# The opening of a two-layer MLP kernel: first weight group loaded and used in pieces between the x tiles, filler bank reused, transposes in two banks

## The chip, the core and the metric

The program runs on one core of one Trainium2 chip. The metric is the device time of one execution in microseconds (us); lower is better. The runs of the kernel before took 876.52 to 876.78 us, with a median of 876.71 us over three.

## What is computed

x has 16 x 512 rows of 768, w1 is 768 x 3072, w2 is 3072 x 768; all of it is float32.

```python
y = np.matmul(x, w1) + b1
y = 0.5 * y * (1.0 + erf(y / np.sqrt(2.0)))
return np.matmul(y, w2).astype(np.float32)
```

## The kernel before, in words

The 8192 rows are cut into pairs of two halves of up to 384 rows. For each pair the kernel forms the hidden values g (first product, bias, Gelu) and then the output (second product). From the second pair on, the first product uses Strassen-like sums with 7 products in place of 8 (function product1, L154), and the second product uses a 15-product scheme (part2, L229). All that needs sums of weights made on the chip. In the opening, where no such sums exist yet, the first pair is computed plainly: w1 is loaded in eight groups of 3 x 128 columns (load_w1), and for each group and half of the rows the function plain (L400) issues six matmuls of 128x384, one for each 128-row chunk of K, into one PSUM bank, and Gelu reads the bank.

PSUM has 8 banks, handed out in turn by bank(), which waits until the earlier user of a bank is done. All matrix instructions run on TensorE (PE) in the order in which the program issues them, since every instruction is recorded as in order.

Before the plain groups 1 to 7 comes the part that the change touches. It handles group 0 of w1 and the six 128-row tiles of x of the first pair:

- x tiles 0 and 1 are loaded by SP's queue as float32 (into xw) and cast to bf16 by DVE and ACT. b1 is loaded on ACT's queue. x tiles 2 to 5 (load_x0) and all weights (load_w1, load_w2) are loaded by POOL's queue, which converts to bf16 on the way. Its order is: x tile 2; chunks 0 to 2 of w1 group 0; then POOL makes the identity matrix (masks.py:197 and 199, cast at L106); chunks 3 to 5 of group 0; x tiles 3, 4, 5; group 1 in two halves; then groups 2 to 7 with the pieces of w2 between them. At most eight of POOL's DMAs are under way: from the ninth on, an issue waits until the DMA eight places ahead of it has landed.
- While nothing has landed, busy(n) (L411) issues n filler matmuls of 128x512 on zeros into a bank pw. There are 9, then 1 and 2 more between the transposes.
- turn_x0(n) (L426) transposes tile n with six PE instructions into a new bank, and DVE copies the result to xt (L104). A small transpose of b1 (L492), copied by ACT, stands between tiles 1 and 2.
- first(n, k0, k1) (L464) multiplies tile n (128 rows) with chunks k0 to k1 of group 0, for its three column blocks: 18 matmuls of 128x128 for one tile with all six chunks. Three tiles of a half share a bank for each column block; Gelu for a half's three banks follows when its last tile is done.

The order on PE is: tiles 0 to 2 transposed, fillers, chunks 0 to 2 for tiles 0 to 2, chunks 3 to 5 for tile 0, transpose of tile 3, chunks 3 to 5 for tiles 1 and 2, transpose of tile 4, tile 3, transpose of tile 5, tile 4, tile 5, then plain.

Of the kernel before, what the change touches and what calls it, by code (L numbers as in the profile page):

```python
# [9 lines left out]
BF16 = mybir.dt.bfloat16  # L10
ACTF = mybir.ActivationFunctionType
ALU = mybir.AluOpType
P = 128
# [20 lines left out]
def kernel(  # L34
# [8 lines left out]
    nc = tc.nc  # L43
# [5 lines left out]
    KC = K // P  # L49
    HC = H // P  # L50
    HP = HC // 2
    KH = KC // 2
    NB = N // 2
    HW = 384
# [20 lines left out]
    def inorder(ins):  # L75
        return tc.keep_in_program_order(ins)

    def dma(queue, out, in_):
        inorder(queue.dma_start(out=out, in_=in_))  # L79
# [9 lines left out]
    xt = keep.tile([P, KC, 2, HW], BF16, name="xt")  # L89
# [5 lines left out]
    b1t = keep.tile([P, HC], FP32, name="b1t")  # L95

    def bank():
        return psp.tile([P, 512], FP32, name="ps")

    def copy(engine, dst, src):  # L100
        if engine == "act":
            inorder(nc.scalar.copy(out=dst, in_=src))  # L102
        elif engine == "dve":
            inorder(nc.vector.tensor_copy(out=dst, in_=src))  # L104
        else:
            inorder(nc.gpsimd.tensor_copy(out=dst, in_=src))  # L106
# [24 lines left out]
    def place_h(hc):  # L131
        h, j = divmod(hc, HP)
        k, q = divmod(j, QH)
        return k * QC + h * QH + q
# [7 lines left out]
    def gelu1(hc, half, src, w, sign):  # L142
        inorder(nc.scalar.activation(out=g[:, place_h(hc), half, :w], in_=src, func=ACTF.Gelu,  # L143
                                     bias=b1t[:, hc:hc + 1], scale=sign))
# [133 lines left out]
    def place(w, n):  # L278
        ns = w // P
        return n // ns, (n % ns) * P  # L280
# [47 lines left out]
    def w1_pair(q):  # L328
        return xftf if HOME[q] is None else w1t[:, HOME[q]:HOME[q] + 2 * GRP]

    def w1_group(gi):
        return w1_pair(gi // 2)[:, gi % 2 * GRP:(gi % 2 + 1) * GRP].rearrange("p (kc c) -> p kc c", kc=KC)

    def load_w1(gi, k0=0, k1=KC):
        c0 = (gi % 2 * HP + gi // 2 * 3) * P
        dma(nc.gpsimd, out=w1_group(gi)[:, k0:k1, :], in_=w1r[:, k0:k1, c0:c0 + 3 * P])
# [70 lines left out]
    pw = bank()  # L407

    def busy(n):
        for _ in range(n):  # L410
            inorder(nc.tensor.matmul(out=pw[:], lhsT=warm[:, 0:P], rhs=warm, start=True, stop=True))  # L411


    def words(ap, first, count):
        return ap[:, 2 * first:2 * (first + count)].bitcast(FP32)
# [4 lines left out]
    def load_x0(n):  # L420
        dma(nc.gpsimd, out=xb0[:, n, :], in_=xf[n * P:(n + 1) * P, :])

    def turn_x0(n, engine):
        pt = bank()[:, :KC * P // 2].bitcast(BF16).rearrange("p (kc c) -> p kc c", kc=KC)
        for kc in range(KC):
            inorder(nc.tensor.transpose(out=pt[:, kc, :], in_=xb0[:, n, kc * P:(kc + 1) * P], identity=ident))  # L426
        half, c0 = place(HW, n)
        copy(engine, xt[:, :, half, c0:c0 + P], pt)

    b1s = words(stf, 2304, P)[:HC, :]  # L430
    ident32 = words(stf, 2432, P)
# [2 lines left out]
    dma(nc.sync, out=xw[:, 1, :], in_=xf[P:2 * P, :])  # L434
    dma(nc.scalar, out=b1s, in_=b1.rearrange("(hc p) -> hc p", p=P))
    load_x0(2)
    load_w1(0, 0, KH)
    inorder(nc.vector.memset(warm, 0.0))
    inorder(nc.scalar.activation(out=b1t[:, 0:1], in_=warm[:, 0:1], func=ACTF.Gelu))
    busy(9)  # L440
    make_identity(nc, ident32)
    copy("pool", ident, ident32)
    load_w1(0, KH, KC)
    for n in range(3, 6):
        load_x0(n)
    load_w1(1, 0, KH)
    load_w1(1, KH, KC)
    load_w1(2)
# [5 lines left out]

    opened = {}

    def first(n, k0=0, k1=KC):
        half, c0 = place(HW, n)
        for hc in range(3):
            if c0 == 0 and k0 == 0:  # L460
                opened[half, hc] = bank()
            ps = opened[half, hc]
            for kc in range(k0, k1):
                inorder(nc.tensor.matmul(out=ps[:, c0:c0 + P], lhsT=w1_group(0)[:, kc, hc * P:(hc + 1) * P],  # L464
                                         rhs=xt[:, kc, half, c0:c0 + P], start=(c0 == 0 and kc == 0),
                                         stop=(kc == KC - 1), skip_group_check=True))
            if c0 == HW - P and k1 == KC:
                gelu1(hc, half, ps[:, :HW], HW, 1.0)

    def groups(p):  # L470
        nonlocal spare, turn
# [11 lines left out]
    EARLY = ("M2a", "M3a")  # L483
    MIDDLE = ("M12", "M2b", "M10a", "M11a", "M11b")

    copy("dve", xb0[:, 0, :], xw[:, 0, :])
    turn_x0(0, "dve")
    copy("act", xb0[:, 1, :], xw[:, 1, :])
    busy(1)
    turn_x0(1, "dve")  # L490
    tb = bank()
    inorder(nc.tensor.transpose(out=tb[:, :HC], in_=b1s, identity=ident32[:HC, :HC]))  # L492
    copy("act", b1t[:], tb[:, :HC])
    turn_x0(2, "dve")
    busy(2)
    for n in range(3):
        first(n, 0, KH)
    first(0, KH, KC)
    turn_x0(3, "dve")
    first(1, KH, KC)  # L500
    first(2, KH, KC)
    for n in range(3, 6):
        if n < 5:
            turn_x0(n + 1, "dve")
        first(n)

    def plains(gi):
        for n in range(3):
# [59 lines left out]
    for p, (r0, w) in enumerate(pairs):  # L568
# [123 lines left out]
        else:  # L692
# [7 lines left out]
            for n, c0, c1 in ((0, 0, NB), (1, 0, NB // 2), (1, NB // 2, NB)):  # L700
                terms = halves[n]
                ps = bank()
                for f, lhs in terms:
                    for c in range(QC):
                        inorder(nc.tensor.matmul(  # L705
                            out=ps[:, :c1 - c0], lhsT=lhs[:, c, :], rhs=w2t[:, c, WF[f], c0:c1],
                            start=(f == terms[0][0] and c == 0), stop=(f == terms[2][0] and c == QC - 1)))
# [33 lines left out]
```

## Time and profile before

| what | value |
|---|---|
| time of the profiled execution | 876.7 us |
| its span (first to last instruction) | 874.9 us |
| median of the runs (lowest, highest) | 876.71 us (876.52, 876.78) |
| PE busy | 868.7 us, 99% of the span |
| DVE, ACT, POOL busy | 591.1, 399.9, 84.4 us |
| first matmul of group 0 (L464) starts | 8.59 us |
| first plain matmul (L400) starts | 16.05 us |

How to read it: all times in the trace count from the first instruction of the span. 1.8 us of the time lie outside the span. A row of the timeline gives the start, the length, the engine, the line, what is written and read, how many instructions are merged, and in brackets how long the engine was idle before it and what ended that. A matmul's end is modelled and lies behind the point at which the next one can start, so the spacing of starts is the better measure of what PE can do. The time to landing of a DMA counts from its issue to the last of its parts being in place.

### The profile page before, as it was taken

The numbers are of one execution on the slowest core, as the hardware profiler recorded it, in microseconds if no ns is written. First come the engines' busy times: TensorE is split into PE (matmuls) and PEld (weight loads), VectorE is DVE, ScalarE is ACT, GpSimd is POOL, SyncE is SP. The second block draws the span as 40 slices with busy tenths as digits, with TensorE's granted clock in tenths as the row PEclk, the third lists the DMA queues.
The fourth block names the chain that finished last, engine by engine and source line by source line (L and its number), as shares of the span: only waits on it lengthen the run. The fifth ranks groups of instructions, "written<-read, shape, count | busy, mean of one in ns | idle before, by whom it ended". The sixth has DMA issues, their size and how long they took to land.

```text
span 874.9 us, 14162 instructions
## 1 busy us (share of the span) xinstructions
PE 868.7 (99%) x5524; PEld 533.8 (61%) x5524; DVE 591.1 (68%) x1110; ACT 399.9 (46%) x792; POOL 84.4 (10%) x153
## 2 busy tenths in 40 slices
PE   8999999999999999999999999999999999999998
PEld 5666566666666666666666666666666666666775
DVE  2889868657856676676577556756765776577654
ACT  3742484167127614731671276147316712751560
POOL 6200110010110001000101100010001011000000
PEclk9999999999999999999999999999999999999999
DMA  9997699276627735671767277366718662771521
GB/s 196 207 209 234 219 324 227 78 204 213 161 64 230 214 89 156 216 170 73 217 204 157 68 240 202 87 166 208 171 71 229 195 153 77 234 196 55 189 88 73
DMA packets 89319, 148.00 MB, mean 169 GB/s; under 512 B 50828, under 2 KB 68388, under 8 KB 89252
## 3 DMA queue, kind: packets, MB, share of 16 engines
q1 hardware_dynamic: 64976, 97.04, 37.2%
q0 software_dynamic: 24096, 49.36, 23.7%
q8 instruction: 43, 0.70, 0.3%
q10 hardware_dynamic: 180, 0.70, 0.2%
q14 instruction: 24, 0.20, 0.1%
HBM read 123.88 MB, written 33.42 MB: 180 GB/s over the span
## 4 chain that ended last, share of the span: by engine, by line
PE 98%; DMA 1%; DVE 0%; POOL 0%; issue 0%; ACT 0%; DVEq 0%; POOLq 0%
PE ps L229 47%; PE ps L154 45%; PE ps L400 5%; PE ps L705 1%; DMA st<-in_x_dram 1%; PE ps L464 0%; POOL w1t L79 0%; PE ps L426 0%; DVE ps L112 0%; DVE ev L112 0%; DVE ev L104 0%; DVE g L112 0%; DVE st L112 0%; POOL st L79 0%; ACT ot L102 0%
## 5 line engine op out<-in xcount | busy, mean ns | idle before, releaser
L154 PEld LDWEIGHTS <-w1t 128*128 128x128 bf16 x2436 | 238.3, 98 | 145.2 <-issue 0.8
L143 ACT ACTIVATE g<-ps,b1t 128x384 bf16<-128x384 f32 (+1 forms) x409 | 221.9, 569 | 89.3 <-PE ps L154 56.8
L154 PE MATMUL ps<-xft,w1t 128*128 128x384 bf16 (+1 forms) x1392 | 259.7, 320 | 0.0
L229 PE MATMUL ps<-w2t,g 128*128 128x384 bf16 x1512 | 257.6, 326 | 0.0
L229 PEld LDWEIGHTS <-g 128*128 128x128 bf16 x1512 | 148.0, 98 | 97.3
L154 PE MATMUL ps<-xt,w1t 128*128 128x384 bf16 (+1 forms) x1044 | 202.3, 320 | 0.1
L109 DVE TENSOR_TENSOR ot<-ot,ps 128x384 f32<-128x384 f32 x231 | 125.5, 552 | 107.4 <-PE ps L229 51.1
L229 PE MATMUL ps<-w2t,st 128*128 128x384 bf16 x1008 | 170.7, 326 | 0.0
L102 ACT COPY ot<-ps 128x384 f32<-128x384 f32 x129 | 60.9, 477 | 220.9 <-PE ps L229 202.6
L229 PEld LDWEIGHTS <-st 128*128 128x128 bf16 x1008 | 98.6, 98 | 65.2
L112 DVE TENSOR_TENSOR ev<-ps,ev 128x384 f32<-128x384 f32 (+1 forms) x119 | 64.7, 544 | 74.6 <-PE ps L154 72.8
L102 ACT COPY ps<-ps 128x384 f32<-128x384 f32 (+1 forms) x119 | 54.0, 454 | 132.9 <-PE ps L154 132.7
L112 DVE TENSOR_TENSOR ps<-ps,ev 128x384 f32<-128x384 f32 (+1 forms) x119 | 65.8, 553 | 44.2 <-PE ps L154 42.1
L104 DVE COPY ev<-ps 128x384 f32<-128x384 f32 (+1 forms) x119 | 64.3, 541 | 22.2 <-PE ps L154 22.0
L143 ACT ACTIVATE g<-ev,b1t 128x384 bf16<-128x384 f32 (+1 forms) x119 | 72.1, 606 | 14.8 <-DVE ev L112 14.7
L112 DVE TENSOR_TENSOR st<-g 128x1024 bf16<-128x1024 bf16 x107 | 73.0, 683 | 1.1 <-ACT g L143 0.9
L79 POOL DMA_DIRECT2D out_dram<-ot x60 | 32.6, 544 | 340.1 <-DVE ot L109 340.1
L112 DVE TENSOR_TENSOR g<-g 128x1024 bf16<-128x1024 bf16 x84 | 57.5, 684 | 0.4
L79 POOL DMA_DIRECT2D xb<-in_x_dram x38 | 20.6, 548 | 341.1 <-DMA xt<-xb 334.3
L400 PE MATMUL ps<-xt,w1t 128*128 128x384 bf16 x204 | 33.8, 326 | 0.0
L109 DVE TENSOR_TENSOR g<-g 128x1024 bf16<-128x1024 bf16 x42 | 29.0, 690 | 1.1
L109 DVE TENSOR_TENSOR st<-st,g 128x1024 bf16<-128x1024 bf16 x42 | 28.9, 688 | 0.8
(73 smaller groups left out, 259.5 us busy)
## 6 DMA issues: line engine op xcount, KB each, us to landing
w1t<-w1f SPq DMA_DIRECT2D x116, 672.0 KB, 5.3
out_dram<-ot POOLq DMA_DIRECT2D x60, 384.0 KB, 2.6
xb<-in_x_dram POOLq DMA_DIRECT2D x38, 192.0 KB, 4.7
w2t<-in_w_dram POOLq DMA_DIRECT2D x8, 576.0 KB, 22.3
ot<-in_x_dram POOLq DMA_DIRECT2D x18, 192.0 KB, 7.7
w1t<-in_w_dram POOLq DMA_DIRECT2D x4, 576.0 KB, 22.2
w1f<-st POOLq DMA_DIRECT2D x3, 672.0 KB, 3.8
w1f<-ot POOLq DMA_DIRECT2D x3, 672.0 KB, 9.1
```

The lines of the kernel that those rows point to most:

```text
L79: inorder(queue.dma_start(out=out, in_=in_))
L102: inorder(nc.scalar.copy(out=dst, in_=src))
L104: inorder(nc.vector.tensor_copy(out=dst, in_=src))
L109: inorder(nc.vector.tensor_tensor(out=dst, in0=a, in1=b, op=ALU.add))
L112: inorder(nc.vector.tensor_tensor(out=dst, in0=a, in1=b, op=ALU.subtract))
L143: inorder(nc.scalar.activation(out=g[:, place_h(hc), half, :w], in_=src, func=ACTF.Gelu, bias=b1t[:, hc:hc + 1], scale=sign))
L154: inorder(nc.tensor.matmul(out=ps[:, :w], lhsT=forms[:, W1F[m], kc, :], rhs=moving1(m, kc, w), start=(kc == 0 and m in ("P1", "P7")), stop ...
L229: inorder(nc.tensor.matmul(out=ps[:, :NB], lhsT=lhs[:, c, :], rhs=w2t[:, c, WF[m], :], start=(m in OPENS and c == 0), stop=(c == QC - 1), ...
L400: inorder(nc.tensor.matmul(out=py[:, :HW], lhsT=lhs[:, kc, (j % 3) * P:(j % 3 + 1) * P], rhs=xt[:, kc, half, :], start=(kc == 0), stop=(kc ...
L705: inorder(nc.tensor.matmul(out=ps[:, :c1 - c0], lhsT=lhs[:, c, :], rhs=w2t[:, c, WF[f], c0:c1], start=(f == terms[0][0] and c == 0), stop= ...
```

## The change

Group 0 of w1 is loaded as five DMAs (chunks 0 and 1 together, then 2, 3, 4, 5 alone) in place of two, and x tiles 3, 4 and 5 are issued between them. The function first now takes a half, a range of its columns (rows of x) and a range of chunks: tiles 0 to 2 are multiplied together, in matmuls of 128x384, chunk by chunk as the pieces arrive; tiles 3 to 5 keep matmuls of 128x128. Nine fillers stay ahead of tile 0, with b1's transpose after the seventh of them; one filler each follows tiles 0 and 1, and two follow tile 2. The filler bank pw becomes the bank of the first sum of half 0. All six tiles are transposed in two fixed banks, turn about; b1's transpose uses a free corner of the second.

```diff
+    turns = (bank(), bank())
+
     def turn_x0(n, engine):
-        pt = bank()[:, :KC * P // 2].bitcast(BF16).rearrange("p (kc c) -> p kc c", kc=KC)
+        pt = turns[n % 2][:, :KC * P // 2].bitcast(BF16).rearrange("p (kc c) -> p kc c", kc=KC)
...
     load_x0(2)
-    load_w1(0, 0, KH)
+    load_w1(0, 0, 2)
     inorder(nc.vector.memset(warm, 0.0))
     inorder(nc.scalar.activation(out=b1t[:, 0:1], in_=warm[:, 0:1], func=ACTF.Gelu))
-    busy(9)
     make_identity(nc, ident32)
     copy("pool", ident, ident32)
-    load_w1(0, KH, KC)
-    for n in range(3, 6):
-        load_x0(n)
+    load_x0(3)
+    load_w1(0, 2, 3)
+    load_w1(0, 3, 4)
+    load_x0(4)
+    load_w1(0, 4, 5)
+    load_x0(5)
+    load_w1(0, 5, 6)
     load_w1(1, 0, KH)
     load_w1(1, KH, KC)
...
-    def first(n, k0=0, k1=KC):
-        half, c0 = place(HW, n)
-        for hc in range(3):
-            if c0 == 0 and k0 == 0:
-                opened[half, hc] = bank()
-            ps = opened[half, hc]
-            for kc in range(k0, k1):
-                inorder(nc.tensor.matmul(out=ps[:, c0:c0 + P], lhsT=w1_group(0)[:, kc, hc * P:(hc + 1) * P],
-                                         rhs=xt[:, kc, half, c0:c0 + P], start=(c0 == 0 and kc == 0),
+    def first(half, c0, c1, k0, k1):
+        if c0 == 0 and k0 == 0:
+            for hc in range(3):
+                opened[half, hc] = pw if half == 0 and hc == 0 else bank()
+        for kc in range(k0, k1):
+            for hc in range(3):
+                inorder(nc.tensor.matmul(out=opened[half, hc][:, c0:c1], lhsT=w1_group(0)[:, kc, hc * P:(hc + 1) * P],
+                                         rhs=xt[:, kc, half, c0:c1], start=(c0 == 0 and kc == 0),
                                          stop=(kc == KC - 1), skip_group_check=True))
-            if c0 == HW - P and k1 == KC:
-                gelu1(hc, half, ps[:, :HW], HW, 1.0)
+        if c1 == HW and k1 == KC:
+            for hc in range(3):
+                gelu1(hc, half, opened[half, hc][:, :HW], HW, 1.0)
...
+    busy(7)
+    tb = turns[1][:, 448:448 + HC]
+    inorder(nc.tensor.transpose(out=tb, in_=b1s, identity=ident32[:HC, :HC]))
+    copy("act", b1t[:], tb)
+    busy(2)
     copy("dve", xb0[:, 0, :], xw[:, 0, :])
     turn_x0(0, "dve")
     copy("act", xb0[:, 1, :], xw[:, 1, :])
     busy(1)
     turn_x0(1, "dve")
-    tb = bank()
-    inorder(nc.tensor.transpose(out=tb[:, :HC], in_=b1s, identity=ident32[:HC, :HC]))
-    copy("act", b1t[:], tb[:, :HC])
+    busy(1)
     turn_x0(2, "dve")
     busy(2)
-    for n in range(3):
-        first(n, 0, KH)
-    first(0, KH, KC)
+    first(0, 0, HW, 0, 2)
     turn_x0(3, "dve")
-    first(1, KH, KC)
-    first(2, KH, KC)
-    for n in range(3, 6):
-        if n < 5:
-            turn_x0(n + 1, "dve")
-        first(n)
+    first(0, 0, HW, 2, 3)
+    first(1, 0, P, 0, 3)
+    first(0, 0, HW, 3, 4)
+    first(1, 0, P, 3, 4)
+    turn_x0(4, "dve")
+    first(0, 0, HW, 4, 5)
+    first(1, 0, P, 4, 5)
+    first(1, P, 2 * P, 0, 3)
+    turn_x0(5, "dve")
+    first(1, P, 2 * P, 3, 5)
+    first(0, 0, HW, 5, 6)
+    first(1, 0, P, 5, 6)
+    first(1, P, 2 * P, 5, 6)
+    first(1, 2 * P, HW, 0, 6)
```

## The prediction

> **What bounds the kernel now.** I read the page's chain first, then PE's waits over the whole span, then the timeline of the first 22 us.
>
> ```profile
> span 874.9 us, 14162 instructions
> ...
> PE 98%; DMA 1%; DVE 0%; POOL 0%; issue 0%; ACT 0%; DVEq 0%; POOLq 0%
> ```
>
> ```profile
> PE ps L411 <- DVE st L438: 1.2, 1, 1.2
> PE ps L464 <- DMA w1t<-in_w_dram: 1.2, 1, 1.2
> PE ps L426 <- ACT st L102: 0.4, 1, 0.4
> PE ps L426 <- DMA st<-in_x_dram: 0.2, 1, 0.2
> ```
>
> The chain that ends last is PE nearly throughout, and PE's only listed waits in 874.9 us (who, for what, total, times, longest) are these four, all in the opening. So the end moves by as much as the first plain matmul (L400, 16.05 us) moves, unless something later becomes late. What sets the 16.05 is in PE's timeline:
>
> ```profile
> 1.19 3.56 PE L411 MATMUL ps<-st 128*128 128x512 bf16 x9 [1.19 <-DVE st L438]
> 4.78 0.51 PE L426 MATMUL ps<-st 128*128 128x128 bf16 x6
> ...
> 5.87 0.51 PE L426 MATMUL ps<-st 128*128 128x128 bf16 x6 [0.37 <-ACT st L102]
> ...
> 6.82 0.59 PE L411 MATMUL ps<-st 128*128 128x512 bf16 x2
> 8.59 2.18 PE L464 MATMUL ps<-xt,w1t 128*128 128x128 bf16 x36 [1.17 <-DMA w1t<-in_w_dram]
> 11.01 0.51 PE L426 MATMUL ps<-st 128*128 128x128 bf16 x6 [0.24 <-DMA st<-in_x_dram]
> ...
> 12.36 0.50 PE L426 MATMUL ps<-st 128*128 128x128 bf16 x6
> ...
> 14.04 2.17 PE L464 MATMUL ps<-xt,w1t 128*128 128x128 bf16 x36
> 16.05 6.01 PE L400 MATMUL ps<-xt,w1t 128*128 128x384 bf16 x36
> 21.90 1.30 PE L400 MATMUL ps<-xt,xft 128*128 128x384 bf16 x7
> ```
>
> Real work starts at 8.59, when half of group 0 has landed. From there PE needs 7.05 us of work and loses 0.41 (36 x 0.0558 after 8.59 is 10.60; the next start is 11.01, when x tile 3 has landed): 8.59 + 7.05 + 0.41 = 16.05.
>
> Durations, by spacing of starts: a 128x128 matmul (16.05 - 14.04)/36 = 0.0558 us; a 128x384 one (21.90 - 16.05)/36 = 0.1625; six transposes 12.70 - 12.36 = 0.34. From the start of a tile's transposes until PE may use it:
>
> ```profile
> 12.90 0.56 DVE L104 COPY xt<-ps 128x768 bf16<-128x768 bf16 x1 [0.78 <-PE ps L426]
> ```
>
> 12.90 + 0.56 - 12.36 = 1.10, and 0.06 to wake PE (DVE's cast ends at 4.72, PE starts at 4.78): **1.16 us**.
>
> **The transfers.** From the second microsecond on the DMA engines always have a backlog: landings follow bytes. POOL's issues, with the times to landing that the trace gives for their windows:
>
> ```profile
> 1.92 0.78 POOL L79 DMA_DIRECT2D w1t<-in_w_dram  x1
> ...
> 3.57 0.79 POOL L79 DMA_DIRECT2D w1t<-in_w_dram  x1
> 4.36 1.65 POOL L79 DMA_DIRECT2D st<-in_x_dram  x3
> 5.98 1.53 POOL L79 DMA_DIRECT2D w1t<-in_w_dram  x2
> ```
>
> ```profile
> DMA to landing us min/median/max: 6.6/7.0/7.4
> ```
>
> The last line is that of the three x tiles. Half 1 of group 0: 1.92 + 6.6 = 8.52 (PE wakes 0.07 later). Half 2: 3.57 + 6.5 = 10.07. x tiles 3 to 5: 4.36 + 6.6 = 10.96, about 11.9, and 12.9. First half of group 1: 5.98 + 8.4 = 14.4; second: 15.8. So 288 KB (bf16 as stored) of w1 take 1.5 us, 192 KB of x 0.95: 0.5 us per 96 KB for both, with nothing visible per DMA (0.95 x 1.5 = 1.43 against 1.5). How a DMA of 96 KB, one chunk, behaves, the trace does not show. Bounds: 0.5 by its bytes, 0.95 if it costs as much as the smallest POOL load shown, an x tile. Less than 0.5 is excluded by the steady rate. I take **0.5**, since two sizes lie on one line through zero.
>
> The pieces then land at: chunks 0 and 1, 8.52 - 0.50 = 8.02; x3 8.97; chunk 2 9.47; chunk 3 9.97; x4 10.92; chunk 4 11.42; x5 12.37; chunk 5 12.87. That is the same total as before (x5 at 12.9), in another order. Issue is no limit: x3 now goes out before half 2 did, three more issues at 0.55 to 0.79 leave POOL free near 8, over 4 us ahead of the data, and the wait for the DMA eight places ahead puts group 1's first half at 8.3 (behind 8.02) in place of 5.98, with four loads of x and w1 still queued. From the load of group 5 on, the issues are those of before (14.66, behind the landing at 14.4).
>
> Queued x tiles land 0.95 us apart, so no DMA here holds up the next by more than that. The Trainium skill (DMA: Bandwidth & Descriptors, section "Anatomy of one DMA — SWDGE (gpsimd) path") speaks against small DMAs: it gives about 2.0 us fixed for each DMA on this path, most of it the wait for the write's receipt, beside bytes at 436 GB/s. If these times followed one another, three more DMAs would by that page of the Trainium skill make an estimated 6 us; by the trace they overlap.
>
> **Edits that cost nothing.** b1's transpose before tile 0: b1's packets are all moved by 3.1 us and the identity it needs is made at 3.28 (2.99 + 0.29), while PE reaches it after seven fillers at about 4.2. It takes 0.17 (6.31 to 6.48) in place of nothing, and tile 0 waits for DVE until 4.78 anyway. If the two fillers behind it still ran at the cold spacing (0.43), tile 0 would start at 5.2; tile 1 still waits for ACT's cast until 5.87, so nothing behind moves. ACT now copies b1t before that cast: done by about 4.9, and the cast waits for its x tile until 4.98. Queued behind it is only the cast; if it were late, tiles 1 and 2 would be late by the same amount, with 0.4 us of cover before 8.09. Two banks for the transposes: each is reused two tiles later, when DVE has long copied it. The filler bank as a sum's bank: PE writes both, in order. The plain groups get their banks back from the last transposes and from half 0's Gelu (now about 14.4 to 16; the third plain bank is wanted at 17.5).
>
> **The sum on PE.** Chunks 0 and 1 on tiles 0 to 2: start 8.02 + 0.07 = 8.09 (tiles 0 to 2 are ready at about 7.6), 6 x 0.1625, to 9.07. x3 landed: transposes to 9.41, tile 3 usable at 9.07 + 1.16 = 10.23. Chunk 2: 9.47 + 0.07 = 9.54 (**0.13 lost**), 0.49, to 10.03. Tile 3, chunks 0 to 2: waits to 10.23 (**0.20 lost**), 9 x 0.0558, to 10.73. Chunk 3: 0.49 + 0.17, to 11.39. Tile 4's transposes, to 11.73, usable 12.55. Chunk 4: 0.49 + 0.17, to 12.39. Tile 4, chunks 0 to 2: waits to 12.55 (**0.16 lost**), to 13.05. Tile 5's transposes, to 13.39. Then 0.34, chunk 5 (0.49 + 0.17 + 0.17), to 14.56, tile 5 usable since 14.21; 18 x 0.0558, to **15.56**. Before: 16.05, so **0.49 us** earlier. The wait for the first half shrinks by 0.50, the one for x3 goes, and 0.49 of new small waits is paid, two of them for the trip through DVE; wide matmuls save 54 x 0.0558 - 18 x 0.1625 = 0.09.
>
> What is late next: group 1's first half, landed at 14.4 (cover 1.2 us). Group 2 landed at 7.50 + 11.3 = 18.8 and is wanted at 21.4; group 7 at 24.78 + 22.9 = 47.7, wanted near 50.7. The instructions after the opening stand in the same order on every engine. So the whole 0.49 should arrive at the end: the profiled time 876.7 (874.9 + 1.8 outside; the median is the same 876.71) less 0.5 is **876.2 us**.
>
> **Rivals.** (1) *Nothing of the new small waits is real*, because pieces land sooner than the slowest of before: PE starts when tiles 0 to 2 are ready, about 7.65, and has 6.95 us of work: 14.6 at the earliest, 1.45 less, 875.25; halfway, 875.7. For it: 2.5 us pass from x tile 2's landing (1.26 + 4.8 = 6.06) to half 1's, 1.0 more than its bytes need, and that loss may not come back. Against: x2 and w1 still meet in that order. 13%.
>
> (2) *Slower: a chunk costs more than its bytes.* With a price p for each of four single chunks, chunk 5 lands at 8.02 + 3 x 0.95 + 4p = 10.87 + 4p, and the end of the opening is 0.07 + 0.49 + 0.34 + 1.00 after it: 12.77 + 4p. That passes 15.56 from p = 0.70 and 16.05 from p = 0.82. At the upper bound 0.95 it gives 16.57, 0.52 later: 877.2. For it: chunks of this size are not in the trace. Against: the line through the two sizes. 13%. Beyond that bound, a fixed time that queued DMAs do not overlap could come on top of the bytes: x tiles land 0.95 apart, so it is at most 0.95, and p at most 0.5 + 0.95 = 1.45, which gives 18.6, 2.5 later: 879.2. From p = 1.26 the loss passes 0.2%. 5%. (By the 2.0 us of the Trainium skill's page DMA: Bandwidth & Descriptors, p = 2.5 would give an estimated 883.4.)
>
> (3) *The opening ends earlier, the kernel does not*, because some later transfer paces PE: 876.7. Against: no listed wait after 11.01. 4%.
>
> The forecast, 876.0 to 876.4 with its small variations, has 65%.
>
> **Chances.** 0.2% is 1.75 us, about what a measurement of this kernel can tell from no change. All but the price above 1.26 lie within it: slower 5%; faster 3% (rival 1 with a gain that I cannot place); same 92%. The range, 875.5 to 877.2, takes in rival 1's middle and rival 2's upper bound and leaves out their ends.
>
> **What would show it.** First L464-like group at about 8.1; the transposes of tile 3 at about 9.1; gaps ahead of tile 3's and tile 4's first matmuls ended by DVE, not DMA; the first plain matmul near 15.6; no new PE wait after it. Landings of single chunks spaced by much over 0.5 would show rival 2; a first start below 7.8, rival 1. Cold spacing (0.43 for a filler, twice 0.0558 for the small ones) anywhere after 5 us would be a mistake of its own.

## The result, and the profile after

The changed kernel takes 878.02 us (median of 22 runs, 875.99 to 880.11) against 876.83 us (median of 22, 876.22 to 877.58): ratio 1.0016, 95% interval 1.0009 to 1.0022. It is slower by about 1.2 us, where 0.5 us faster was forecast; the time lies outside the forecast range of 875.5 to 877.2. The difference is within the 0.2% that the forecast called no change, but the interval excludes 1. One of the 22 runs took 875.99 us; it was not profiled.

The profiled execution took 877.77 us. Its span, its PE busy row and its chain:

```profile
span 876.0 us, 14098 instructions
...
PE 869.9 (99%) x5489; PEld 533.3 (61%) x5489; DVE 590.9 (67%) x1110; ACT 400.1 (46%) x792; POOL 85.9 (10%) x156
...
PE 97%; DVE 1%; DMA 1%; ACT 0%; issue 0%; SPq 0%; DVEq 0%
```

The span grew by 1.1 us (876.0 against 874.9). DVE has come into the chain, and the DMA in it is now a write to DRAM (w1f<-st, below) in place of the load of an x tile. PE's waits over the whole span (engine, line, for what, total, times, longest):

```profile
PE ps L229 <- DVE ot L109: 1.3, 1, 1.3
PE ps L411 <- DVE st L440: 1.2, 1, 1.2
PE ps L468 <- DVE xt L104: 0.4, 2, 0.2
```

The waits for w1 and x in the opening are gone, as intended. A new one of 1.3 us stands in the second product (L229), far from every edited line.

**The opening ends about where it was forecast to.** PE's timeline:

```profile
5.34 0.85 PE L428 MATMUL ps<-st 128*128 128x128 bf16 x6
...
8.21 1.14 PE L468 MATMUL ps<-xt,w1t 128*128 128x384 bf16 x6 [0.22 <-DVE xt L104]
...
10.33 1.32 PE L468 MATMUL ps<-xt,w1t 128*128 128x128 bf16 x15 [0.16 <-DVE xt L104]
...
15.63 6.01 PE L400 MATMUL ps<-xt,w1t 128*128 128x384 bf16 x36
```

The first plain matmul starts at 15.63 (forecast 15.56, before 16.05): 0.42 us earlier. ACT's first Gelu of the plain groups starts at 17.78 against 18.20, and DVE's first addition of the second product (L109) at 65.81 against 66.23: still 0.42 earlier, 50 us later. Then it turns round. In DVE's timeline the kernel before has

```profile
72.27 1.48 DVE L109 TENSOR_TENSOR ot<-ot,ps 128x384 f32<-128x384 f32 x3
73.89 0.69 DVE L112 TENSOR_TENSOR st<-g 128x1024 bf16<-128x1024 bf16 x1
74.50 0.55 DVE L109 TENSOR_TENSOR ot<-ot,ps 128x384 f32<-128x384 f32 x1
```

and the changed one

```profile
71.86 1.48 DVE L109 TENSOR_TENSOR ot<-ot,ps 128x384 f32<-128x384 f32 x3
75.07 0.69 DVE L112 TENSOR_TENSOR st<-g 128x1024 bf16<-128x1024 bf16 x1 [1.73 <-DMA w1f<-st]
```

DVE arrives 0.41 earlier and leaves 1.18 later. It may not write to the buffer st before the write of a formed piece of w1 from st to DRAM (w1f<-st, issued on SP's queue) has landed. The chain after shows the whole path:

```profile
70.04 4.94 DMA w1f<-st
...
75.07 0.69 DVE st L112
75.76 0.47 DVE ot L109
76.23 0.04 issue
76.28 5.85 PE ps L229 x35
```

PE's rows at that place, in the kernel before

```profile
73.90 10.56 PE L229 MATMUL ps<-w2t,g 128*128 128x384 bf16 x64
```

and in the changed one

```profile
73.48 1.46 PE L229 MATMUL ps<-w2t,g 128*128 128x384 bf16 x8
76.28 9.26 PE L229 MATMUL ps<-w2t,g 128*128 128x384 bf16 x56 [1.34 <-DVE ot L109]
```

The eight matmuls ahead of the wait start at 73.48, so PE could have gone on at 73.48 + 8 x 0.1625 = 74.78; it goes on at 76.28, 1.50 later. 1.50 - 0.42 = 1.08, which is the 1.1 us of the span, and nearly all later rows of DVE and ACT stand 1.08 later than before.

From the landing to PE's next matmul, by way of DVE's two rows, 1.31 us pass (74.97 to 76.28). The kernel before had little to spare here: its write landed at 73.80, which by the same 1.31 lets PE go on at 75.11, and PE itself came to that matmul at 73.90 + 8 x 0.1625 = 75.20. So the slack was an estimated 0.09 us, and it showed in no list of waits.

The write was issued 0.49 us earlier than before (70.04 against 70.53) and landed 1.17 later (74.97 against 73.80). The DMA queues and issues of 71.0 to 72.6 us of the changed kernel name what else was there:

```profile
q1 hardware_dynamic: 108, 0.58, 96.9%
q8 instruction: 1, 0.02, 5.6%
```

The second row is one packet of 16 KB on a queue of kind "instruction". In the records of the packets it starts at 71.11 and takes 1.43 us; in those of the landing, fifteen of the write's sixteen parts are in by 73.31, and the sixteenth comes at 74.97. In the kernel before that packet starts at 67.7, ahead of the write, and all sixteen parts land between 73.60 and 73.80. Had the last part come with the others, PE could by the 1.31 us have gone on at an estimated 74.62, ahead of its own 74.78, and the 0.42 would have passed this place whole. Over the run there are 43 such packets in either kernel, about 20.5 us apart: as many as PE's 11,000 instructions have blocks of 256, so I take them for the fetches of PE's instructions. The changed opening has 18 wide matmuls in place of 54 narrow ones and one filler more: with the weight loads, PE's program is 70 rows shorter (10979 against 11049), so each fetch comes at a later point of the work.

About half of the 0.49 us by which the write is issued earlier has the same cause. The write stands behind two x transposes on SP's queue, in the kernel before

```profile
67.57 2.78 SPq L287 DMA_TRANSPOSE xt<-xb  x2
```

and in the changed one

```profile
67.31 2.54 SPq L287 DMA_TRANSPOSE xt<-xb  x2
```

In the kernel before the fetch (67.7) starts inside the first of the two, which takes 1.45 us in place of 1.21; the rest is the start, 0.26 apart. In three of the ten profiles of this case a fetch starts inside that transpose, and it takes 1.45 to 1.98 us; in the other seven it takes 1.21. So the kernel before, too, had a fetch in the chain that leads to this write. That the fetch makes the transpose longer is inferred from the times.

### The profile page after: what moved, and what is told of

The parts are those of the page before. It is cut to its first block, busy times and chain, and to the rows that moved or that the text cites. A ratio compares the mean times of both kernels' runs of the same rounds, so it can differ in the third digit from the quotient of the medians.

```text
span 876.0 us, 14098 instructions
## 1 busy us (share of the span) xinstructions
PE 869.9 (99%) x5489; PEld 533.3 (61%) x5489; DVE 590.9 (67%) x1110; ACT 400.1 (46%) x792; POOL 85.9 (10%) x156
## 4 chain that ended last, share of the span: by engine, by line
PE 97%; DVE 1%; DMA 1%; ACT 0%; issue 0%; SPq 0%; DVEq 0%
PE ps L229 45%; PE ps L154 44%; PE ps L400 5%; PE ps L719 1%; PE ps L468 1%; DMA w1f<-st 1%; PE ps L411 1%; DVE ot L109 0%; PE ps L428 0%; ACT ot L102 0%; DVE st L112 0%; DVE xt L104 0%; DVE st L109 0%; DVE ps L112 0%; DVE ev L112 0%
## 5 line engine op out<-in xcount | busy, mean ns | idle before, releaser
L229 PE MATMUL ps<-w2t,g 128*128 128x384 bf16 x1512 | 257.8, 326 | 1.3 <-DVE ot L109 1.3
L229 PEld LDWEIGHTS <-g 128*128 128x128 bf16 x1512 | 147.9, 98 | 98.8 <-issue 1.6
L109 DVE TENSOR_TENSOR ot<-ot,ps 128x384 f32<-128x384 f32 x231 | 125.4, 552 | 106.9 <-PE ps L229 51.4
L229 PE MATMUL ps<-w2t,st 128*128 128x384 bf16 x1008 | 170.7, 326 | 0.0
L229 PEld LDWEIGHTS <-st 128*128 128x128 bf16 x1008 | 98.6, 98 | 65.2
L109 DVE TENSOR_TENSOR g<-g 128x1024 bf16<-128x1024 bf16 x42 | 29.0, 690 | 1.1
L109 DVE TENSOR_TENSOR st<-st,g 128x1024 bf16<-128x1024 bf16 x42 | 28.9, 688 | 0.8
```

Source lines behind the costliest of these rows:

```text
L109: inorder(nc.vector.tensor_tensor(out=dst, in0=a, in1=b, op=ALU.add))
L229: inorder(nc.tensor.matmul(out=ps[:, :NB], lhsT=lhs[:, c, :], rhs=w2t[:, c, WF[m], :], start=(m in OPENS and c == 0), stop=(c == QC - 1), ...
```

## The theories and the experiments

- **Theory A**: the fetch's place follows PE's instruction count. By losing 70 rows the change moved one fetch into the write w1f<-st; the one of the 16 DMA engines that serves both makes the write land some 1.4 us late, and DVE and PE wait.
- **Theory B**: the write is slow because it is issued 0.5 us earlier, into other traffic.
- **Theory C**: the new order of PSUM banks, or something else in the new opening, makes PE wait for DVE.

Times in this section are medians of 11 or 12 runs; the kernel before has 876.73 on the chip of the first four and 876.67 on that of the last four. The changed kernel was not run again there; it is 1.19 us behind the kernel before that ran beside it.

### The instruction count back, by narrow matmuls

```diff
-                inorder(nc.tensor.matmul(out=opened[half, hc][:, c0:c1], lhsT=w1_group(0)[:, kc, hc * P:(hc + 1) * P],
+                for c in range(c0, c1, P):
+                    inorder(nc.tensor.matmul(out=opened[half, hc][:, c:c + P], lhsT=w1_group(0)[:, kc, hc * P:(hc + 1) * P],
...
```

> The changed kernel, but the multiplications of tiles 0 to 2 are issued as three matmuls of 128x128 in place of one of 128x384: PE's instruction count is again that of before to within two rows (11051, against 11049 before and 10979 in the changed kernel), everything else is as in the changed kernel, and PE's work grows by 0.09 us. Theory A (PE's fetch of a 16384-byte block of instructions, a single packet on one DMA engine, now falls into the write of w1f<-st, makes that engine and so the landing 1.4 to 1.6 us late, and DVE and then PE wait for it): the fetch goes back to about 67.5 us, ahead of the write; w1f<-st lands about 0.4 us earlier than before (near 73.4), no listed PE wait near 75, and the time is 876.83 - 0.42 + 0.09 = about 876.5. Theory B (the write is late because it is issued 0.5 us earlier, into other traffic): the wait of about 1.3 us stays, time about 878.1. Theory C (the new order of PSUM banks or another part of the new opening makes PE wait for DVE): the wait stays, about 878.1.

Measured: 876.82 us, ratio 1.0004 (0.9995 to 1.0012). PE's second largest wait is down:

```profile
PE ps L229 <- DVE ot L109: 0.6, 1, 0.6
```

The fetch is at 66.7 in this profile, ahead of the write, and the write takes 3.3 us from issue, as before. It is issued later, though, at 71.02: the fetch now hits the load of the last x tile, and SP's x transposes, which wait for that load, stand ahead of the write. The write lands at 74.32, not near the 73.4 expected. The time is 0.09 us behind the kernel before, against 1.19 for the changed kernel, so 1.1 of the 1.5 us expected were regained. The wait that C expects to stay is mostly gone. On B this run says little: the write was issued later than before, so B's own condition is not met. What speaks against B is the changed kernel's trace, where fifteen parts land 3.27 us after the issue (70.04 to 73.31), just as the whole write does before (70.53 to 73.80), and the next run.

### The instruction count alone, in the kernel before

```diff
-    for n in range(3):
-        first(n, 0, KH)
-    first(0, KH, KC)
+    wide(0, KH + 1)
     turn_x0(3, "dve")
-    first(1, KH, KC)
-    first(2, KH, KC)
+    wide(KH + 1, KC)
```

wide(k0, k1) multiplies tiles 0 to 2 together in matmuls of 128x384.

> The kernel before, with one edit: tiles 0 to 2 are multiplied by group 0 in matmuls of 128x384 (18 in place of 54). The loads, their order, the banks and the transposes stay as before, and PE has 72 instruction rows fewer (10977). Theory A: although the opening ends at nearly the same time (0.09 us earlier at most), the fetch moves to about 71 us or later, w1f<-st lands near 75, PE waits about 1 to 1.5 us for DVE near 75, and the time is 876.83 - 0.1 + 1.0 to 1.5 = 877.7 to 878.3. Theories B and C: no wait, 876.7 to 876.8.

Measured: median 877.95, but in two groups: five runs at 876.47 to 877.01 and six at 877.95 to 878.20; ratio over all 1.0006 (0.9997 to 1.0015). The one profiled run (876.64) is of the first group. There the write w1f<-st is issued at 69.93, earlier than in the changed kernel, and fifteen of its parts are in by 73.21, 3.28 us later: an early issue does not make it slow, and B is out. The fetch starts at 73.28, just after that; the sixteenth part lands at 73.82, and the fetch hits the next write, w1f<-ev: fifteen of its parts are in by 74.88, the last at 76.67. DVE waits until 73.92 (0.33 us listed), PE has no listed wait after 11. The groups lie 1.3 us apart by their medians (876.76 and 878.08), which is what A expects of a fetch that falls a little earlier in some runs; no run of the second group was profiled.

### The write taken out of the way

```diff
     waiting.pop(0)(nc.scalar)
+    waiting.pop(0)(nc.scalar)
```

> The changed kernel, with the write of w1f<-st issued on ACT's queue right after w1f<-ot, ahead of the x transposes, in place of after them on SP's queue. It then lands well ahead of DVE's next use of st near 73.5, whatever a fetch does to it. Theories A and B: no PE wait near 75; the 0.42 us gained in the opening reach the end: about 876.4. If the next write (w1f<-ev) is what then holds ACT, it shows as an ACT wait, not a PE wait. Theory C: the wait stays, about 878.

Measured: 876.06 us, ratio 0.9995 (0.9987 to 1.0003); eleven of twelve runs lie between 875.78 and 876.37, and 876.37 is the fastest of 35 runs of the kernel before. The fetch is where it was (71.1), and it now holds up the x transposes, which nobody on PE waits for. PE's waits and DVE's row at the place in question:

```profile
PE ps L411 <- DVE st L440: 1.2, 1, 1.2
PE ps L468 <- DVE xt L104: 0.4, 2, 0.2
```

```profile
71.81 1.48 DVE L109 TENSOR_TENSOR ot<-ot,ps 128x384 f32<-128x384 f32 x3
73.20 0.68 DVE L112 TENSOR_TENSOR st<-g 128x1024 bf16<-128x1024 bf16 x1
```

No gap between the two, and with the banks and the opening as in the changed kernel PE does not wait here: C is out. The opening ends at 15.58, and the 0.47 us that ACT and DVE gain there are still 0.40 at the last Gelu (845.25 against 845.65). This is the fastest version measured, though its interval just includes 1.

### The same write early, in the kernel before

The edit is the same line.

> The kernel before, with the same edit as the one before this: w1f<-st issued early on ACT's queue. A control for the edit alone. In the kernel before, DVE's next write to st starts 0.09 us after the landing, so little was lost there: all theories expect 876.7 to 876.9, within 0.1 us of before. A clear gain here would mean that the kernel before also lost time at this place.

Measured: 876.52, ratio 0.9997 (0.9988 to 1.0005). Some 0.2 us lower in the median, a little more than the 0.1 expected, and not told apart from before: the early write does not explain the gain of the changed kernel by itself.

### The instruction count back, at no cost in time

```diff
+            pieces = 4 if split else 1
...
+            for i in range(pieces):
+                inorder(nc.tensor.matmul(out=pw[:, i * s:(i + 1) * s], lhsT=warm[:, 0:P], rhs=warm[:, i * s:(i + 1) * s],
+                                         start=True, stop=True))
```

> The changed kernel with one edit that costs PE no time: twelve of the thirteen fillers of 128x512 are issued as four of 128x128 each, on the same zeros into the same bank. PE's instruction count goes from 10979 to 11051 rows, that of before to within two. The opening, the loads and the write stay as in the changed kernel. Theory A (the instruction fetch, placed by PE's instruction count, delays w1f<-st): the fetch goes back from 71.1 to about 67 us, and the time falls from 878.0 to between 876.4 (nothing left of the wait) and 876.8 (as in the run with narrow matmuls, where the fetch hit the x loads ahead of the write and some 0.6 us of the wait stayed). Theory B (earlier issue of the write): 878.0.

Measured: 876.75, ratio 1.0000 (0.9991 to 1.0008). The fetch is at 67.7; the write is issued at 70.70 and lands evenly, its sixteen parts between 73.79 and 73.99. A shorter wait is left:

```profile
74.08 0.69 DVE L112 TENSOR_TENSOR st<-g 128x1024 bf16<-128x1024 bf16 x1 [0.63 <-DMA w1f<-st]
```

```profile
PE ps L400 <- DMA w1t<-in_w_dram: 0.4, 1, 0.4
PE ps L229 <- DVE ot L109: 0.2, 1, 0.2
```

Splitting fillers adds instructions and no work (four of 128x128 take 0.43 us at the cold spacing, as one of 128x512 does), and it takes back 1.1 us: 0.08 behind the kernel before, against 1.19. What is left of the wait is not free of the fetch either: as in the kernel before, the fetch starts inside SP's x transposes, which take 2.95 us, and the write is issued 0.66 later than in the changed kernel. The first of the two PE waits is the same mechanism at another place: an earlier fetch, at 13.6 in this profile, falls into the load of group 1's first half, of which fifteen parts are in by 14.18 and the last at 15.69 (7.79 + 7.9), in place of 13.9 (7.93 + 6.0) in the changed kernel.

### Half way

The same edit with six fillers split.

> The same with six fillers split: 11015 rows, half way. Theory A: the fetch falls near 69 us, into the x transposes that stand on the same DMA engines just ahead of the write; the held-up engine starts the write late, but part of the time is over before the write begins: time between those of the other two, 876.6 to 877.6, with single runs possibly in two groups, since the fetch's place moved by up to 2 us between kernels of equal count. Theory B: 878.0.

Measured: 876.83 (876.12 to 877.74), ratio 1.0002 (0.9993 to 1.0011). The fetch is at 69.6, in the x transposes; the write lands at 74.03, DVE waits 0.9 us for it and PE 0.5. As A expects, the rest of PE's wait is between the other two (0.2 and 1.3). The time is not told apart from that with twelve fillers split (876.75), so it is the profile that supports A here.

### The pieces joined again

```diff
     load_x0(3)
-    load_w1(0, 2, 3)
-    load_w1(0, 3, 4)
+    load_w1(0, 2, 4)
     load_x0(4)
-    load_w1(0, 4, 5)
     load_x0(5)
-    load_w1(0, 5, 6)
+    load_w1(0, 4, 6)
```

on top of the early write.

> The changed kernel with the early write of w1f<-st on ACT's queue (so that the opening's time reaches the end), and with the single chunks of group 0 joined again: chunks 2 and 3 in one DMA after x tile 3, chunks 4 and 5 in one DMA after x tiles 4 and 5. It tells what the pieces alone are worth. By the durations of the forecast: chunk 5 lands as before, chunk 4 then lands with it at about 12.5, 1 us later than alone, so PE, which needs chunk 4 ahead of tile 4's first chunks, waits about 0.6 to 0.8 us at about 11.8; the first plain matmul starts at about 16.2 and the time is about 876.7, against 876.06 with the pieces. If pieces cost more than their bytes (rival 2 of the forecast), joining them gains instead: below 876.0.

Measured: 877.27, ratio 1.0007 (0.9999 to 1.0016). PE's timeline:

```profile
12.60 1.33 PE L466 MATMUL ps<-xt,w1t 128*128 128x384 bf16 x15 [0.50 <-DMA w1t<-in_w_dram]
...
16.27 0.98 PE L400 MATMUL ps<-xt,w1t 128*128 128x384 bf16 x5
```

The expected wait for chunk 4 is there, and the first plain matmul starts at 16.27 (expected 16.2), 0.69 later than with single chunks. Of this 0.17 is there from the first matmul of group 0 on (8.33 against 8.16), so the single chunks are worth about 0.5 us in the opening. The time, 0.6 us above what I expected, is only partly explained: I had set it down as 876.7 for an opening that ends 0.2 us later than before, which should have read 876.9; and by the last Gelu the profile is 0.37 behind the kernel before (846.02 against 845.65) where the opening left it 0.22 behind. The other 0.15 comes in two steps, near 124 and 281 us, and was not traced further; the second, of 0.09, is also in the kernel before with the early write.

### Both: early write and the count back

> The early write of w1f<-st together with the split fillers (11051 rows): the fetch is at about 67 us and the write is out of its way wherever it falls. If the fetch costs PE time through that write alone, this equals the kernel with the early write: 876.0 to 876.2. If the fetch also costs PE time elsewhere, it differs from it by more than 0.2 us.

Measured: 876.32, ratio 0.9995 (0.9986 to 1.0004). Beside the padded kernel without the early write (876.75) that is 0.43 us less: what the opening gains, 0.42, was eaten by the same write even with the fetch in the transposes ahead of it. Beside the early write alone it is 0.26 higher, more than the 0.2 that the expectation allowed, but the two ran on different chips and are not told apart. By the profiles the fetch costs no more here: the first plain groups are 0.38 ahead of the kernel before, against 0.47 with the early write alone, and the last Gelu 0.30 against 0.40; there is no listed PE wait after 11 us either.

## Why the prediction was wrong, point by point

**What bounds the kernel** (PE, and the end moves with the first plain matmul "unless something later becomes late"): right as a statement; the exception is what happened.

**The transfers**: right. The pieces landed at 7.6, 9.1, 9.6, 11.1 and 12.5 (issue plus time to landing: 1.94 + 5.7, 4.09 + 5.0, 4.74 + 4.9, 5.79 + 5.3, 6.95 + 5.6), each about 0.4 ahead of the forecast, and the x tiles alike (8.6, 10.6, 12.0). In the kernel before, the last of a load's sixteen parts was some 0.65 us behind the others (7.89 and 8.54 for half 1), and the 8.52 from which the forecast counts contains it; here it is 0.35 behind at first (8.74 and 9.09 for chunk 2) and not at all from x tile 4 on (10.54 and 10.57). Why is open. So rival 1's ground, that a loss of before may not come back, came true in part. (The backlog of the DMA engines stands from about 3 us on, not from the second microsecond: their busy share is 0.66 from 2 to 3 us and 1.05 from 3 to 4.) The steps between the single chunks, 0.5 us where one follows the other, give p = 0.5: rival 2 did not happen. The fixed 2.0 us that the Trainium skill (DMA: Bandwidth & Descriptors, section "Anatomy of one DMA — SWDGE (gpsimd) path") gives for each DMA overlap here, as the trace of before had shown.

**The edits at no cost**: right but for one. In this run the fillers stayed at the cold spacing beyond the point where b1's transpose stands, and tile 0 was transposed at 5.34 in 0.64 us. The forecast had allowed for cold fillers but not for cold transposes behind them, though it named cold spacing after 5 us as a mistake of its own. Tile 2 was ready only at 8.2 (forecast 7.6), so PE started at 8.21 though chunk 1 was there at 7.6. That this is near the forecast 8.09 is luck: the loads were 0.4 us early and the tiles 0.6 late. In the run with twelve fillers split, where the full spacing came earlier, PE started at 7.80.

**The sum on PE**: right from its start on. By the spacing of starts PE loses 0.33 us ahead of tile 3 (forecast 0.13 + 0.20; chunk 2 was already there, so all of it is the trip through DVE) and 0.16 ahead of tile 4 (forecast 0.16). The start is 0.12 late and was set by DVE's copy of tile 2 (0.22 listed), not by chunk 1 as forecast. The gain is 0.42 against 0.49.

**What is late next: the step that failed.** It said: "The instructions after the opening stand in the same order on every engine. So the whole 0.49 should arrive at the end." For that I had checked loads only, the groups of w1. I had not gone through the writes to DRAM that free a buffer. One of them, w1f<-st, landed at 73.80 in the kernel before, and DVE's next instruction on that buffer started at 73.89 after 0.14 us of idleness, a gap too short for the list of waits; PE's slack there was 0.09 us. Its time hangs on a chain of DMAs (x tiles loaded, transposed on SP's queue, then the write), which in these profiles issues it between 69.93 and 71.02 whatever PE gained. That is the mechanism of rival 3, which I gave 4% on the ground that no wait was listed after 11.01; an unlisted wait is not slack. But rival 3 priced it at the gain alone, and what came is a wait of 1.50 us on PE, 1.08 more than the gain. With the fetch out of the write, though still in the transposes ahead of it (split fillers), the first Gelu of the plain groups is 0.31 ahead of before (17.89 against 18.20), the last Gelu of all 0.09 behind (845.74 against 845.65): 0.4 us go here, and the gain with them. What this place costs when no fetch falls near it no run shows; by the estimate above, nothing in the changed kernel.

**What no part of the forecast had**: that the number of instructions is itself a quantity the change moves. The page's row "q8 instruction: 43" was in front of me, as was the count of 5524 matmuls. Without it, no rival of the forecast makes a late write cost more than the gain. The runs put its price at 1.1 us, by the distance from the kernel before that ran beside each: 1.19 for the changed kernel, 0.08 with the count restored by split fillers and 0.09 with it restored by narrow matmuls. The two groups of runs, 1.3 apart, when 72 rows are taken from the kernel before, fit this. It is shown by the count alone being changed, by the packet's place in the traces, and by the one late part in sixteen. That the fetch and the late part share one DMA engine is inferred from their times; the records do not name the engine.

Left open: why the fetch's place differs by up to 2 us between kernels of nearly equal count (71.1 and 73.3; at 20.5 us per 256, some 70 rows are an estimated 5.6 us, and from 67.7 it moved by 3.4 and 5.6), and so whether a given run is hit; and what parts the runs with the early write into 875.8 to 875.9 and 876.2 to 876.4.

## What to carry to other kernels

After an early gain, look for the first buffer that is freed by a DMA rather than by the engine that gained, and work out its slack from the rows: when it lands, what follows on the engines behind it, and when the engine that bounds the kernel needs that. A gap too short for the list of waits can mean that there is next to none (0.09 us here). Count the instructions that a change adds or takes away on PE: in these runs each block of 256 was a 16 KB transfer, beside which the load, transpose or write under way came late, and a write is as late as the latest of its sixteen parts. Moving the tight transfer early (one line; from 1.19 us behind the kernel before to 0.67 ahead of it in the median) is a surer cure than moving the fetch, whose place varies between kernels of equal count and, by the two groups of times above, probably from run to run.

## What the runs showed of the hardware

- While one 16 KB packet of instructions was moved (1.43 us), one part of a 672 KB write came 1.66 us behind the other fifteen (73.31 and 74.97), which kept their time. The same shows in a load (14.18 and 15.69, with split fillers). The Trainium skill (Runtime: NRT & Kernel Launch, section "Instruction fetch mechanics") gives blocks of 16 KiB, 256 instructions, fetched ahead by the sequencer's own DMA queue, and calls the cost mostly hidden. The trace agrees on the size and the interval. PE's lists of waits name none for an instruction, so it is hidden from PE here too. What it costs is paid by the data beside it.
- The moment at which PE's full clock was granted differed from profile to profile with the same start of fillers at 1.19 us. The traces record it at 4.15 us in the kernel before and at 6.62 in the changed one, and at 4.37 and 6.43 in two variants of the kernel before. The spacing of the fillers falls from 0.43 to 0.22 us near 4.2 in the kernel before, and the transposes of the changed kernel run at 0.107 us each until about 6.6, then at 0.056. That the Trainium skill (TensorE: Matmul & The Clock Gate, section "What's actually happening") says too: the window that decides it runs free of the kernel's start.
